# A two-layer transformer trunk: one more pair in block products, weight tiles rounded by DMA, and a new order of the steps

## The chip, the cores and the metric

The kernel runs on one core of one Trainium2 chip. The metric is the device time of one execution in microseconds (us), taken as the median of several executions. The profile is one execution taken by the hardware profiler; its time stands apart, and it lists every instruction of the engines: TensorE (PE, with PEld for its weight loads), VectorE (DVE), ScalarE (ACT), GpSimd (POOL) and SyncE (SP).

## What is computed

Two layers over 256 tokens of 1024 features in float32. Each layer is an attention (the first over 16 heads, causal; the second over 12 heads in three dilated windows), then a squared-ReLU MLP, each followed by a residual and a layer norm:

```python
def sq_relu_mlp(x, w_in, w_out):
    return jnp.square(jax.nn.relu(x @ w_in)) @ w_out      # 1024 -> 4096 -> 1024
...
for i in range(DEPTH):                                     # DEPTH = 2
    mix = moba_attention(...) if i % 2 == 0 else dilated_attention(...)
    h = layer_norm(DEEPNORM_ALPHA * h + mix, ln_mix_g[i], ln_mix_b[i])
    h = layer_norm(DEEPNORM_ALPHA * h + sq_relu_mlp(h, mlp_w_in[i], mlp_w_out[i]), ln_mlp_g[i], ln_mlp_b[i])
```

All weights (about 100 MB) are read from HBM once per execution, and nothing of them is kept between executions.

## The kernel before, in words

**Three products for one.** TensorE multiplies in a rounded form of float32 (fp32r). To keep the accuracy, each operand is split in two: `hi` is the operand rounded to fp32r, `lo` is what is left, `operand - hi`. A product then takes three matmuls: hi·hi, hi·lo and lo·hi. So each 128x1024 weight tile (512 KB) needs work ahead of TensorE: a DMA into a `raw` buffer on SP's queue, a copy that rounds on ACT (`whi<-raw`), and a subtraction on DVE (`wlo<-raw,whi`). There are 7 buffers `raw`, 10 `whi` and 10 `wlo`. Tiles that are named in `FAR` (and in `FAR_W` outside the steps of the MLPs) go without the subtraction: ACT writes `-hi` into `wlo` and a second DMA, on POOL's queue, adds the weights to it from HBM (`far_parts`, L422 to L425).

**The MLP.** The 4096 hidden units are 16 pairs of 128-column tiles. Pairs 0 and 1 are computed at the head (`relu_sq_tok`). For each other pair `p`, two steps `f p 0` and `f p 1` (`do_first`) load a tile of `w_in` each, multiply it, and put the two precision halves together (`half_sum`, L1124); then `square` takes relu and square with two ACT instructions. Then comes the second factor, for which a pair is of one of two kinds:

- A plain pair (`o`, or `O`, which splits its activations early) loads two tiles of `w_out` and takes 2 tiles x 2 token halves x 2 column halves x 3 = 24 matmuls of 128x512 (`do_out`, `mm_rows`).
- A pair in block products (`a`, or `A`, which makes its sums early) takes seven products of blocks in place of eight (Winograd's form of Strassen's scheme), 7 x 3 = 21 matmuls of 128x512 (`do_duo`, `mm_duo`). For this DVE makes four sums of activation blocks (`duo_sums`, L749 on 128x128) and four sums of weight blocks (`load_duo`, L749 on 128x512), and splits the sums like other operands. For a pair in `BY_DMA` two of the four weight sums are one adding DMA of POOL (L698). Its second half runs at the step `b`.

After the last block pair, step `z` (`combine`) adds the partial products to the residual; the pairs behind `z` are the tail, whose products are held back and ordered so that the layer norm of one token half lies beside the products of the other.

**What sets the order.** The program doesn't issue instructions as it is written. Each operation is recorded with a cost, and a list scheduler (`Plan.order`) fixes the order of each engine's queue; the strings `STEPS` give the order in which the MLP's steps are recorded. Buffers that hold finished activations until their step comes are called cells (`CELLS`, `BIG`: parts of attention's tiles that lie idle in the MLP).

On the chip each engine works through its queue in order. POOL's queue holds the adding DMAs and also one small power function per layer norm (`rstd`, L1009), so a DMA that waits there holds up a layer norm behind it.

The pairs in block products are, before: 10 in the first MLP (2, 3, 4, 6, 7, 8, a, c, d, e in hexadecimal) and 11 in the second (2, 3, 4, 5, 6, 7, a, b, c, d, e).

Of the kernel before, what the change touches and what calls it, by code (L numbers as in the profile page):

```python
# [7 lines left out]
F32 = mybir.dt.float32  # L8
# [3 lines left out]
ALU = mybir.AluOpType  # L12
# [29 lines left out]
)  # L42
BY_DMA = ({2, 6, 8, 14}, {2, 5, 6, 10, 14})
FAR = (
    {("f", 7, 0), ("f", 10, 1), ("f", 12, 0), ("f", 12, 1), ("f", 14, 1), ("o", 1, 1), ("s", 6, 0), ("s", 10, 0)},
    {("f", 2, 1), ("f", 7, 0), ("f", 11, 0), ("f", 14, 1), ("s", 10, 0), ("s", 14, 0)},
)
FAR_W = {0, 12, 14, 16, 21, 32, 34, 35, 36, 39, 43, 48, 53, 57}
GB_AT, MASK_AT = "fc1", "f21"
SQUARES = ("AAAAAAAAAAAAAAAA", "AAAAAAAAAAAAAAAA")  # L50


def kinds_of(i):
    at = {int(x[1], 16): x[0] for x in STEPS[i].split() if x[0] in "oOaA"}
    return ["sS"["aA".index(at[p])] if at[p] in "aA" else at[p] for p in range(DFF // 256)]
# [89 lines left out]
class Plan:  # L145
# [52 lines left out]
    def order(self):  # L198
# [40 lines left out]
        def start_of(o):  # L239
# [9 lines left out]
            for tag, bs in need.items():  # L249
# [8 lines left out]
                s = max(s, sorted(slots[tag])[len(bs) - 1])  # L258
# [3 lines left out]
        while len(done) < total:  # L262
# [64 lines left out]
DMA_ISSUE, DMA_FETCH, DMA_LANDS, DMA_RING = 1.0, 2.0, 8.4, 6  # L327
# [20 lines left out]
def tile_trunk(  # L348
# [73 lines left out]
    def far_parts(raw, hi, lo, src, keys):  # L422
        op("ACT", act(1024, sbuf=True), lambda: nc.scalar.activation(hi.t, raw.t, AF.Copy), keys, [(hi, 0)])  # L423
        op("ACT", act(1024, sbuf=True), lambda: nc.scalar.activation(lo.t, f32(hi.t), AF.Copy, scale=-1.0), [(hi, 0)], [(lo, 0)])  # L424
        op("POOL", DMA_ISSUE, lambda: nc.gpsimd.dma_start(lo.t, src, accum_op=ALU.add), (), [(lo, 0)], xfer=P * 1024 * 8)  # L425

    def load_far(src):

        w = W()
        w.raw = mk([P, 1024], F32, "raw", NRAW)  # L430
        w.hi = mk([P, 1024], F32R, "whi", NHI)
        w.lo = mk([P, 1024], F32R, "wlo", NLO)
        dma(lambda: w.raw.t, src, (), [(w.raw, 0)], P * 1024 * 4)
        far_parts(w.raw, w.hi, w.lo, src, [(w.raw, 0)])
        return w
# [3 lines left out]
    def load_w(src):  # L439
        loads[0] += 1  # L440
        return (load_far if loads[0] - 1 in FAR_W else load_near)(src)

    def load_near(src, n=1024):
        w = W()
        w.raw = mk([P, 1024], F32, "raw", NRAW)
        w.hi = mk([P, 1024], F32R, "whi", NHI)
        w.lo = mk([P, 1024], F32R, "wlo", NLO)
        dma(lambda: w.raw.t[:, :n], src[:, :n], (), [(w.raw, 0)], P * n * 4)
        split(
            n, lambda: w.raw.t[:, :n], lambda: w.hi.t[:, :n], lambda: w.lo.t[:, :n],  # L450
            [(w.raw, 0)], [(w.hi, 0)], [(w.lo, 0)], sbuf=True,
        )
        return w

# [205 lines left out]
    def duo_sums(u, cells):  # L660

        t, c0, _ = u
# [14 lines left out]
    def load_duo(pair, single, by_dma, far):  # L677
# [8 lines left out]
        def wide(t, src=None):  # L686
            h, l = [mk([P, 1024], F32R, tag, n) for tag, n in (("whi", NHI), ("wlo", NLO))]
            if src is not None:
                far_parts(t, h, l, src, [(t, 0), (t, 1)])
                return [(h, l, c, 0) for c in (0, 512)]  # L690
            split(1024, lambda: t.t, lambda: h.t, lambda: l.t, [(t, 0), (t, 1)], [(h, 0)], [(l, 0)], sbuf=True)
# [3 lines left out]
        w3, w2 = wide(y, pair[:, 1024:] if far else None)  # L695
# [9 lines left out]
        w5, w7 = wide(x)  # L705
        tt(512, y0, y0, x0, ALU.add, yk[:1] + xk[:1], yk[:1])
        tt(512, y1, y1, y0, ALU.add, yk, yk[1:])
        w6, w4 = wide(y)
# [431 lines left out]
    def relu_sq_tok(ps, m, ahi, alo):  # L1140
# [5 lines left out]
        t = slice(m * P, (m + 1) * P)  # L1146
        keys = [(j, m) for j in range(4)]
        split(
            512, lambda: pt.t.rearrange("p (j s) -> p j s", j=4), lambda: ahi.t[:, :, t], lambda: alo.t[:, :, t],
# [3 lines left out]
    class Mlp:  # L1153
# [17 lines left out]
        def rest(self, between):  # L1171
# [12 lines left out]
            nduo = sum(k in "sS" for k in kinds)  # L1184
# [443 lines left out]
```

## Time and profile before

| | |
|---|---|
| median of 3 executions | 546.9 us (546.07 to 547.66) |
| the profiled execution | 548.12 us, of which the span from the first to the last instruction is 546.3 us |
| granted TensorE clock, mean | 0.996 |
| busy in the span: PE, DVE, ACT, POOL | 537.5, 476.1, 389.8, 41.7 us |
| DMAs moved | 125.03 MB |
| DMAs issued by SP for `w_in` and `w_out` | 64 and 64 |
| DMAs issued by POOL | 37 |

How to read it: the first attention runs to about 105 us of the span, the first MLP to about 290, the second attention to about 360, and the second MLP to 539; the last layer norm and the stores follow. A busy PE is one that has matmuls in flight. The chain of waits follows the end of the program back, at each step to what released the instruction; in a list of groups, a row gives line, engine, operation, tiles (written <- read), shape and count, then busy time in us and the mean of one in ns, then idle time just before them.

### The profile page before, as it was taken

What the parts mean: (1) busy time and instruction counts of PE and PEld (TensorE: products, weight loads), DVE (VectorE), ACT (ScalarE), POOL (GpSimd) and SP (SyncE); (2) the same over time, 40 slices, a digit from 0 to 9 for tenths busy, and PEclk for the clock granted to TensorE, in tenths of its full rate; (3) what the DMA queues carried; (4) which work ended last, traced back from release to release, by engine and by line L of the source; (5) the groups of instructions that cost most, each with busy time, mean ns of one, the idle gap of its engine ahead of it and who ended that gap; (6) DMA issues with size and microseconds to landing.
All of it is one profiled execution on the core that took longest, in us unless ns stands there. A gap on an engine that the chain in (4) does not pass through costs nothing.

```text
span 546.3 us, 8734 instructions
## 1 busy us (share of the span) xinstructions
PE 537.5 (98%) x3172; PEld 458.5 (84%) x3172; DVE 476.1 (87%) x846; ACT 389.8 (71%) x613; POOL 41.7 (8%) x52
## 2 busy tenths in 40 slices
PE   9999999999999999999999999999999999999994
PEld 7989888888888878888888889888888888888884
DVE  6679998897899899899857789879889899899997
ACT  6558999278799768798645558746876997877530
POOL 0000010010001000100011000110010100100001
PEclk9999999999999999999999999999999999999998
DMA  8987787929869879979998756865894989885602
GB/s 331 343 328 242 190 196 197 382 88 308 229 155 237 279 220 288 225 182 324 338 252 224 253 179 173 246 201 138 277 278 118 227 280 268 261 202 178 215 24 78
DMA packets 35611, 125.03 MB, mean 229 GB/s; under 512 B 3952, under 2 KB 4848, under 8 KB 35568
## 3 DMA queue, kind: packets, MB, share of 16 engines
q1 hardware_dynamic: 29664, 104.35, 55.9%
q0 software_dynamic: 5328, 19.40, 19.7%
q10 hardware_dynamic: 576, 0.72, 0.4%
q8 instruction: 25, 0.41, 0.3%
q14 instruction: 18, 0.15, 0.1%
HBM read 123.40 MB, written 1.05 MB: 228 GB/s over the span
## 4 chain that ended last, share of the span: by engine, by line
PE 94%; DVE 2%; DMA 2%; ACT 0%; issue 0%; POOL 0%; DVEq 0%; POOLq 0%; ACTq 0%
PE acc L417 59%; PE tp L417 32%; PE tp L890 3%; DMA raw<-in_win_dram 2%; DVE wlo L413 1%; ACT whi L408 0%; DVE raw L749 0%; POOL rstd L1004 0%; DVE tok L756 0%; DVEq L1622 0%; DVE ta L749 0%; DVE ta L413 0%; DVE pt L413 0%; DVE bst L1035 0%; ACT ta L1127 0%
## 5 line engine op out<-in xcount | busy, mean ns | idle before, releaser
L413 DVE TENSOR_TENSOR wlo<-raw,whi 128x1024 fp32r<-128x1024 f32 (+2 forms) x200 | 222.8, 1137 | 22.1 <-ACT whi L408 20.2
L408 ACT ACTIVATE whi<-raw 128x1024 fp32r<-128x1024 f32 (+2 forms) x198 | 191.0, 995 | 49.8 <-PE acc L417 14.4
L417 PE MATMUL acc<-xs,whi 128*128 128x512 f32 (+1 forms) x496 | 113.4, 374 | 1.1 <-DVE q0lo L749 1.1
L417 PEld LDWEIGHTS acc<-xs,whi 128*128 128x128 f32 x496 | 87.1, 191 | 17.8 <-DVE q0lo L749 1.5
L417 PEld LDWEIGHTS acc<-xs,wlo 128*128 128x128 f32 x448 | 60.0, 191 | 3.5 <-issue 0.2
L417 PE MATMUL acc<-xs,wlo 128*128 128x256 f32 x448 | 62.5, 283 | 0.0
L417 PE MATMUL tp<-xs,whi 128*128 128x512 f32 x224 | 56.3, 392 | 0.0
L417 PE MATMUL acc<-whi,ahi 128*128 128x512 f32 (+1 forms) x130 | 49.7, 392 | 0.0
L417 PEld LDWEIGHTS tp<-xs,whi 128*128 128x128 f32 x224 | 40.4, 189 | 7.3
L417 PE MATMUL acc<-wlo,ahi 128*128 128x512 f32 (+1 forms) x109 | 42.3, 388 | 0.0
L423 ACT ACTIVATE whi<-raw 128x1024 fp32r<-128x1024 f32 x28 | 29.5, 1053 | 16.4 <-PE acc L417 15.3
L417 PE MATMUL acc<-whi,alo 128*128 128x512 f32 (+1 forms) x108 | 39.3, 388 | 0.0
L417 PEld LDWEIGHTS tp<-xs,wlo 128*128 128x128 f32 x224 | 30.5, 190 | 2.1
L417 PE MATMUL tp<-xs,wlo 128*128 128x256 f32 x224 | 31.5, 283 | 0.0
L424 ACT ACTIVATE wlo<-whi 128x1024 fp32r<-128x1024 f32 x28 | 29.6, 1058 | 0.4
L417 PE MATMUL acc<-whi,xs 128*128 128x512 f32 (+1 forms) x112 | 29.0, 364 | 0.0
L417 PEld LDWEIGHTS acc<-whi,ahi 128*128 128x128 f32 x130 | 24.4, 188 | 5.0 <-issue 0.3
L749 DVE TENSOR_TENSOR ta<-acc,ta 128x256 f32<-128x256 f32 x41 | 17.0, 421 | 12.1 <-ACT ta L777 8.7
L417 PE MATMUL tp<-whi,xs 128*128 128x512 f32 x80 | 25.4, 396 | 0.0
L417 PE MATMUL acc<-whi,ta 128*128 128x512 f32 (+1 forms) x72 | 24.5, 384 | 0.0
L417 PEld LDWEIGHTS acc<-whi,alo 128*128 128x128 f32 x108 | 20.3, 188 | 4.2
L417 PEld LDWEIGHTS acc<-wlo,ahi 128*128 128x128 f32 x109 | 20.5, 188 | 3.8
(246 smaller groups left out, 947.8 us busy)
## 6 DMA issues: line engine op xcount, KB each, us to landing
raw<-in_win_dram SPq DMA_DIRECT2D x64, 512.0 KB, 5.7
raw<-in_wout_dram SPq DMA_DIRECT2D x64, 512.0 KB, 6.1
raw<-in_wqk_dram SPq DMA_DIRECT2D x22, 512.0 KB, 8.9
raw<-in_wo_dram SPq DMA_DIRECT2D x14, 512.0 KB, 5.3
wlo<-in_win_dram POOLq DMA_DIRECT2D x10, 512.0 KB, 9.2
raw<-in_wout_dram POOLq DMA_DIRECT2D x9, 512.0 KB, 8.5
raw<-in_wv_dram SPq DMA_DIRECT2D x8, 512.0 KB, 5.4
wlo<-in_wqk_dram POOLq DMA_DIRECT2D x7, 512.0 KB, 9.2
```

Of the source, the lines that this page charges most:

```text
L408: op("ACT", act(n, sbuf=sbuf), lambda: nc.scalar.activation(hi(), src(), AF.Copy), r, whi)
L413: lambda: nc.vector.tensor_tensor(lo(), src(), f32(hi()), op=ALU.subtract), list(r) + list(whi), wlo,
L417: nc.tensor.matmul(out_ap, lhsT, rhs, start=start, stop=stop)
L423: op("ACT", act(1024, sbuf=True), lambda: nc.scalar.activation(hi.t, raw.t, AF.Copy), keys, [(hi, 0)])
L424: op("ACT", act(1024, sbuf=True), lambda: nc.scalar.activation(lo.t, f32(hi.t), AF.Copy, scale=-1.0), [(hi, 0)], [(lo, 0)])
L749: op("DVE", dve(n) + extra, lambda: nc.vector.tensor_tensor(out_ap(), a(), b(), op=alu), r, w)
L890: nc.tensor.transpose(ps.t[:, c : c + P], src(), ident.t)
```

## The change

- The first MLP takes pairs 3, 4, 5, 6, 7, 8, 9, a, b, c, d in block products (11), the second takes 2, 4, 5, 6, 8, 9, a, b, c, d, e (11). Three of them are of a new kind `M`: like `A`, with two of their cells in the buffer `m1` (attention's mask), which is loaded later than before. A kind `G` is added too and is not used.
- A tile in `CAST` or `CAST_W` gets its `hi` from a DMA of POOL that rounds on the way (`cast_in`); ACT's copy goes. There are 42 such tiles. A tile in `FAR` or `FAR_W` gets its `lo` from ACT's `-hi` and an adding DMA as before. A tile in both (15) has no `raw` buffer and no DMA of SP. Three adding DMAs add a sum of weight blocks and read it from SBUF (`wlo<-raw`).
- `BY_DMA` shrinks from 4 and 5 pairs to 2 and 1. `TWICE` would take all four weight sums by DMA; no pair is in both sets, so it doesn't act.
- Seven pairs (`D` in `SQUARES`) take relu and square in one DVE instruction in place of two of ACT.
- `STEPS` has a new order in both MLPs; the planner hands out buffers first in, first out, and has two other constants for DMAs of POOL.

```diff
-    "f20 fd0 f21 f30 fc0 f40 f31 f41 fa0 fd1 f80 fa1 f90 A4 f50 f81 f51 Aa Ad fc1 ba f70 bd b4 A2 fb0 f91 "
+    "f40 f80 f30 f31 f41 fa0 fa1 f81 A3 fd0 fc0 f90 b3 fd1 A4 fc1 M8 f20 fb0 b4 f91 ff0 f70 f71 b8 Aa ff1 "
...
-BY_DMA = ({2, 6, 8, 14}, {2, 5, 6, 10, 14})
+BY_DMA = ({9, 10}, {5})
...
-FAR_W = {0, 12, 14, 16, 21, 32, 34, 35, 36, 39, 43, 48, 53, 57}
-GB_AT, MASK_AT = "fc1", "f21"
-SQUARES = ("AAAAAAAAAAAAAAAA", "AAAAAAAAAAAAAAAA")
+FAR_W = {13, 17, 28, 30, 38, 55, 57}
+GB_AT, MASK_AT = "f91", "bb"
+CAST = (
+    {("f", 2, 1), ("f", 4, 1), ("f", 5, 1), ("f", 12, 0), ("f", 13, 0), ("o", 14, 1)},
...
+CAST_W = {12, 13, 15, 17, 18, 24, 27, 28, 30, 33, 34, 36, 37, 40, 42, 43, 45, 47, 53, 54, 55, 56}
+TWICE = ({5, 12, 13}, {4, 6, 7, 9, 11, 12, 13, 14})
+SQUARES = ("AAAADAAAADDAAAAD", "AAAADAAAAAAAADAD")
...
-                s = max(s, sorted(slots[tag])[len(bs) - 1])
+                s = max([s] + slots[tag][: len(bs)])
...
-    def far_parts(raw, hi, lo, src, keys):
-        op("ACT", act(1024, sbuf=True), lambda: nc.scalar.activation(hi.t, raw.t, AF.Copy), keys, [(hi, 0)])
+    def cast_in(hi, src):
+        op("POOL", DMA_ISSUE, lambda: nc.gpsimd.dma_start(hi.t, src), (), [(hi, 0)], xfer=P * 1024 * 4 - 1)
+
+    def add_in(lo, hi, src, keys=()):
         op("ACT", act(1024, sbuf=True), lambda: nc.scalar.activation(lo.t, f32(hi.t), AF.Copy, scale=-1.0), [(hi, 0)], [(lo, 0)])
-        op("POOL", DMA_ISSUE, lambda: nc.gpsimd.dma_start(lo.t, src, accum_op=ALU.add), (), [(lo, 0)], xfer=P * 1024 * 8)
+        op("POOL", DMA_ISSUE, lambda: nc.gpsimd.dma_start(lo.t, src(), accum_op=ALU.add), keys, [(lo, 0)], xfer=P * 1024 * 8)
...
+    def load_as(src, far, cast):
 
         w = W()
-        w.raw = mk([P, 1024], F32, "raw", NRAW)
+        if not (far and cast):
+            w.raw = mk([P, 1024], F32, "raw", NRAW)
         w.hi = mk([P, 1024], F32R, "whi", NHI)
         w.lo = mk([P, 1024], F32R, "wlo", NLO)
-        dma(lambda: w.raw.t, src, (), [(w.raw, 0)], P * 1024 * 4)
-        far_parts(w.raw, w.hi, w.lo, src, [(w.raw, 0)])
+        if not (far and cast):
+            dma(lambda: w.raw.t, src, (), [(w.raw, 0)], P * 1024 * 4)
+        if cast:
+            cast_in(w.hi, src)
+        else:
+            op("ACT", act(1024, sbuf=True), lambda: nc.scalar.activation(w.hi.t, w.raw.t, AF.Copy), [(w.raw, 0)], [(w.hi, 0)])
+        if far:
+            add_in(w.lo, w.hi, lambda: src)
+        else:
+            low_part(w.raw, w.hi, w.lo, [(w.raw, 0)])
         return w
...
+    def low_part(raw, hi, lo, keys):
+        tt(1024, lambda: lo.t, lambda: raw.t, lambda: f32(hi.t), ALU.subtract, [*keys, (hi, 0)], [(lo, 0)])
...
-                    n = {"O": 2, "S": 4}.get(kinds[p], 0)
-                    u = cells.take(F32) if not n else (mk([P, 512], F32, "ta", NTA), 0, 0)
-                    homes = [cells.take(F32R, True) for _ in range(n)]
+                    n = {"O": 2, "S": 4, "M": 2}.get(kinds[p], 0)
+                    u = cells.take(F32) if kinds[p] in "os" else (mk([P, 512], F32, "ta", NTA), 0, 0)
+                    homes = [h for tag in {"G": ("g", "b"), "M": ("m1",)}.get(kinds[p], ()) for h in cells.spot(tag)]
+                    homes += [cells.take(F32R, True) for _ in range(n)]
```

Two places show what this does to the queues. The first is POOL's queue where the second MLP begins, around the two `rstd` of the layer norm ahead of it. `whi<-in_win` is a rounding DMA of a tile of `w_in`, `wlo<-in_win` an adding one, `in_wout` is `w_out`. Before:

```order
L425 DMA wlo_793_4102<-in_win_dram 128x1024
L1009 TENSOR_TENSOR rstd_779_4182<-rstd_779_4182,expo_3_100 128x1
L425 DMA wlo_817_4196<-in_win_dram 128x1024
L1009 TENSOR_TENSOR rstd_801_4245<-rstd_801_4245,expo_3_100 128x1
L698 DMA raw_919_4482<-in_wout_dram 128x1024
L425 DMA wlo_922_4628<-in_wout_dram 128x1024
```

And now:

```order
L429 DMA whi_785_4003<-in_win_dram 128x1024
L433 DMA wlo_783_4083<-in_win_dram 128x1024
L433 DMA wlo_789_4103<-in_win_dram 128x1024
L429 DMA whi_805_4132<-in_win_dram 128x1024
L1039 TENSOR_TENSOR rstd_776_4168<-rstd_776_4168,expo_3_100 128x1
L429 DMA whi_812_4176<-in_win_dram 128x1024
L429 DMA whi_824_4188<-in_win_dram 128x1024
L1039 TENSOR_TENSOR rstd_797_4228<-rstd_797_4228,expo_3_100 128x1
L429 DMA whi_871_4348<-in_win_dram 128x1024
L429 DMA whi_896_4464<-in_win_dram 128x1024
L433 DMA wlo_872_4514<-in_win_dram 128x1024
```

One adding DMA stood between the two `rstd`; now two rounding DMAs stand there, and a further one right ahead of the first.

The second place is DVE's queue near the end of the first MLP. Rows `wlo<-raw,whi` take the low part of a weight tile, rows `raw<-raw` sum weight blocks, `tok` is the residual. Before, plain pairs come last here:

```order
L413 TENSOR_TENSOR wlo_569_2964<-raw_567_2855,whi_568_2944 128x1024
L413 TENSOR_TENSOR wlo_572_2974<-raw_570_2872,whi_571_2952 128x1024
L413 TENSOR_TENSOR wlo_575_2984<-raw_573_2903,whi_574_2966 128x1024
L413 TENSOR_TENSOR wlo_580_2993<-raw_578_2915,whi_579_2986 128x1024
L413 TENSOR_TENSOR ta_577_3005<-pt1_368_2100,ta_576_2959 128x512
L413 TENSOR_TENSOR wlo_583_3017<-raw_581_2929,whi_582_3000 128x1024
L749 TENSOR_TENSOR ta_584_3015<-tp_371_2255,ta_584_3015 128x512
```

And now, from the last but one block pair on:

```order
L779 TENSOR_TENSOR raw_552_2745<-raw_552_2745,raw_551_2718 128x512
L419 TENSOR_TENSOR wlo_556_2928<-raw_562_2797,whi_555_2884 128x512
L779 TENSOR_TENSOR wlo_565_2938<-raw_563_2815,whi_564_2895 128x1024
L419 TENSOR_TENSOR q0hi_497_2950<-ta_495_2782,v_496_2930 128x512
L419 TENSOR_TENSOR ta_561_2952<-ta_557_2888,ta_560_2940 128x384
L779 TENSOR_TENSOR raw_552_2745<-raw_552_2745 128x512
L779 TENSOR_TENSOR wlo_567_2961<-raw_551_2718,whi_566_2942 128x1024
L779 TENSOR_TENSOR raw_562_2797<-raw_562_2797 128x512
L779 TENSOR_TENSOR raw_562_2797<-raw_562_2797,raw_563_2815 128x512
L779 TENSOR_TENSOR wlo_569_2980<-raw_552_2745,whi_568_2963 128x1024
L779 TENSOR_TENSOR raw_563_2815<-raw_563_2815,raw_562_2797 128x512
L779 TENSOR_TENSOR raw_563_2815<-raw_563_2815 128x512
```

The sums of weight blocks, four to a pair, stand close to the end of the MLP now, between the low parts. Over the whole program, by the queues: DVE goes from 810 rows to 840, ACT from 563 to 504, POOL's DMAs from 37 to 72, SP's from 203 to 188. TensorE's matmuls of 128x512 go from 1725 to 1722, the others stay.

More of the change, by code (lines that the diff above doesn't have):

```diff
@@ L623, in __init__ @@
             self.half = []
+            self.gone = set()
         def take(self, dtype, wide=False):
@@ L684, in load_duo, with wide @@
         dma(lambda: y.t, pair[:, 1024:], (), yk, P * 1024 * 4)
-        def wide(t, src=None):
+        def wide(t, part, src, again):
             h, l = [mk([P, 1024], F32R, tag, n) for tag, n in (("whi", NHI), ("wlo", NLO))]
[L688 to L691, printed above, removed]
+            keys = [(t, 0), (t, 1)]
+            if part in cast:
+                cast_in(h, src)
+            else:
+                op("ACT", act(1024, sbuf=True), lambda: nc.scalar.activation(h.t, t.t, AF.Copy), keys, [(h, 0)])
+            if part in far:
+                add_in(l, h, again, [] if src is not None else keys)
+            else:
+                low_part(t, h, l, keys)
             return [(h, l, c, 0) for c in (0, 512)]
         split(512, x0, part(hi, q * 512, 512), part(lo, q * 512, 512), xk[:1], [(hi, q)], [(lo, q)], sbuf=True)
-        w3, w2 = wide(y, pair[:, 1024:] if far else None)
+        w3, w2 = wide(y, 0, pair[:, 1024:], lambda: pair[:, 1024:])
         if by_dma:
@@ L704, in load_duo @@
         yield w2, w3, (hi, lo, q * 512, q)
[L705 to L708, printed above, removed]
+        w5, w7 = wide(x, 1, None, lambda: x.t)
+        if by_dma > 1:
+            op(
+                "POOL", DMA_ISSUE, lambda: nc.gpsimd.dma_start(y1(), pair[:, :512], accum_op=ALU.add), yk[1:], yk[1:],
+                xfer=P * 512 * 8,
+            )
+            op("POOL", DMA_ISSUE, lambda: nc.gpsimd.dma_start(y.t, x.t, accum_op=ALU.add), xk + yk, yk, xfer=P * 1024 * 8)
+        else:
+            tt(512, y0, y0, x0, ALU.add, yk[:1] + xk[:1], yk[:1])
+            tt(512, y1, y1, y0, ALU.add, yk, yk[1:])
+        w6, w4 = wide(y, 2, None, lambda: y.t)
         yield w5, w7, w6, w4
@@ L1146, in relu_sq_tok @@
         t = slice(m * P, (m + 1) * P)
+        quads = lambda tile: tile.rearrange("p (j s) -> p j s", j=4)
+        if alo is None:
+            op(
+                "ACT", act(512), lambda: nc.scalar.activation(quads(ahi.t)[:, :, t], quads(pt.t), AF.Copy), [pt],
+                [(ahi, j) for j in range(4)],
+            )
+            return
         keys = [(j, m) for j in range(4)]
         split(
-            512, lambda: pt.t.rearrange("p (j s) -> p j s", j=4), lambda: ahi.t[:, :, t], lambda: alo.t[:, :, t],
+            512, lambda: quads(pt.t), lambda: ahi.t[:, :, t], lambda: alo.t[:, :, t],
             [pt], [(ahi, k) for k in keys], [(alo, k) for k in keys],
@@ L1160, in head @@
             self.ws = [[load_w(win[i][c * 4 + j]) for j in range(4)] for c in range(nx)]
-            self.chunks = {c: act_tiles() for c in range(nx)}
+            whole = kinds_of(i)[0] in "sS"
+            self.chunks = {c: (mk([P, 1024], F32, "ahi", 3), None) if whole else act_tiles() for c in range(nx)}
             self.half(0)
@@ L1183, in rest @@
             prods = []
-            nduo = sum(k in "sS" for k in kinds)
+            nduo = sum(k in "sSGM" for k in kinds)
             single = [None]
@@ L1219, in do_first @@
                     square(held[p][0], SQUARES[i][p])
-                    if kinds[p] in "OS":
+                    if kinds[p] in "OSGM":
                         ready(p)
@@ L1226, in do_pair @@
             def do_pair(p):
-                if p < 2 * nx:
+                if kinds[p] in "os" and p in held:
+                    ready(p)
+                if p < 2 * nx and kinds[p] == "o":
                     gets = [rows_of(*chunks[p // 2], p % 2 * 2 + k) for k in range(2)]
                 else:
-                    if kinds[p] in "os":
-                        ready(p)
                     gets = held[p]
@@ L1257, in do_duo @@
                 a11, a12, a22, s1, s2, s3, s4 = do_pair(p)
-                weights = load_duo(wout[i][p], (*single[0], q), p in BY_DMA[i], ("s", p, 0) in FAR[i])
+                weights = load_duo(wout[i][p], (*single[0], q), (p in BY_DMA[i]) * (1 + (p in TWICE[i])), *[
+                    {n for n in range(3) if ("s", p, n) in parts[i]} for parts in (FAR, CAST)
+                ])
                 if q:
@@ L1295, in combine @@
                 tt(512, lambda: z1.t[:, hi], w(p5), lambda: z1.t[:, hi], ALU.add, [(z1, 1), p5], [(z1, 1)])
+            if chunks[0][1] is None:
+                for p in range(2 * nx):
+                    homes = [cells.take(F32R, True) for _ in range(4)] if kinds[p] == "S" else []
+                    held[p] = (chunks[0][0], p * 512, 2 * p), homes
+                    taken[p] = homes
+                    if homes:
+                        ready(p)
             late_ = False
@@ L1570, in _layout @@
         for p, kind in enumerate(kinds_of(i)):
-            if kind in "sS":
+            if kind in "sSGM":
                 t = wo[i, p // 2, p % 2, 1]
```

58 lines of the change are left out of this document (29 added, 29 removed), and 6 rows, old and new, of the table STEPS.

## The prediction

> **What bounds the kernel now.** I read the page's totals first, then what TensorE waits for, then the chain of waits, then busy time by stage. On the page:
>
> ```profile
> span 546.3 us, 8734 instructions
> PE 537.5 (98%) x3172; PEld 458.5 (84%) x3172; DVE 476.1 (87%) x846; ACT 389.8 (71%) x613; POOL 41.7 (8%) x52
> ```
>
> TensorE is busy for all but 8.8 us of the span. The list of TensorE's own waits has two rows:
>
> ```profile
> PE acc L417 <- DVE q0lo L749: 1.1, 1, 1.1
> PE tp L417 <- PEq L1613: 0.8, 1, 0.8
> ```
>
> One of them is the start. The other, 1.1 us, is the only time in the program's middle at which TensorE had nothing to do, for a result of DVE. The chain of waits (start, length, what) shows where it lies and where the end lies:
>
> ```profile
> 172.44 10.45 DMA raw<-in_win_dram
> ...
> 194.51 0.35 DVE q0lo L749
> ...
> 194.90 3.06 PE acc L417 x16
> ...
> 217.40 0.68 PE tp L417 x3
> 218.08 2.77 PE acc L417 x16
> ...
> 539.34 0.44 DVE bst L1035
> ```
>
> So up to 539.3 us TensorE sets the end, but for one detour: a load of a `w_in` tile that took 10.45 us, then ACT and DVE work until 194.9, in the first MLP. The 7 us behind 539.3 are the last layer norm and the stores, whose code doesn't change. This fixes the best that can come: less TensorE work, and the one wait.
>
> The stages (busy us of each engine and instruction count in each stretch, then granted clock, DMA share and GB/s), first the two MLPs whole, then parts of them:
>
> ```profile
> 122.00:287.00 165.00, 163.94 (x832) 139.27 (x832) 144.97 (x220) 128.76 (x180) 14.03 (x16) 1.00 0.86 252
> 378.00:539.00 161.00, 161.00 (x833) 137.96 (x833) 149.22 (x231) 115.39 (x166) 9.61 (x11) 1.00 0.71 208
> ```
> ```profile
> 160.00:200.00 40.00, 38.94 (x198) 32.86 (x197) 36.89 (x60) 33.47 (x48) 3.47 (x4) 1.00 0.78 228
> ...
> 378.00:420.00 42.00, 42.00 (x240) 36.85 (x240) 37.82 (x62) 31.37 (x48) 1.75 (x2) 1.00 0.80 230
> 420.00:460.00 40.00, 40.00 (x204) 34.15 (x204) 37.01 (x59) 37.71 (x56) 3.48 (x4) 1.00 0.88 248
> 460.00:500.00 40.00, 40.00 (x204) 34.12 (x203) 36.73 (x61) 31.32 (x47) 3.45 (x4) 1.00 0.81 227
> 500.00:539.00 39.00, 39.00 (x190) 32.83 (x189) 37.66 (x52) 15.00 (x17) 0.93 (x1) 1.00 0.36 122
> ```
>
> DVE (third busy figure) is the next engine behind TensorE: 88% in the first MLP, 93% in the second, 97% in its last 39 us, there without a wait of TensorE. ACT has room, DMA some.
>
> **The change part by part.**
>
> *Products.* A plain pair takes 24 matmuls of 128x512 and a block pair 21. Block pairs go from 10 to 11 in the first MLP and stay 11 in the second, so three matmuls go. The chain has three of them in 0.68 us at 217.40. They lie on TensorE, which sets the end: -0.7 us, certain if TensorE still sets it.
>
> *The wait at 194 us.* The new order of steps may take it away (-1.1) or leave one of its kind.
>
> *DVE and ACT.* The groups by shape give busy us and mean ns of one:
>
> ```profile
> L413 DVE TENSOR_TENSOR wlo<-raw,whi 128x1024 fp32r<-128x1024 f32 x171 | 205.0, 1220 | 19.9 <-ACT whi L408 18.5 <-PE acc L417 0.5
> L749 DVE TENSOR_TENSOR raw<-raw,raw 128x512 f32<-128x512 f32 x33 | 22.6, 686 | 0.3
> L749 DVE TENSOR_TENSOR ta<-ta,ta 128x128 f32<-128x128 f32 x34 | 9.8, 287 | 0.4
> L756 DVE SCALAR_TENSOR_TENSOR tok<-tok,ta 128x512 f32<-128x512 f32 x6 | 4.1, 686 | 0.1
> L413 DVE TENSOR_TENSOR alo<-ta,alo 128x384 fp32r<-128x384 f32 x6 | 3.3, 553 | 0.3 <-ACT alo L408 0.3
> ```
> ```profile
> L408 ACT ACTIVATE whi<-raw 128x1024 fp32r<-128x1024 f32 x171 | 175.9, 1056 | 47.4 <-PE acc L417 14.4 <-PE tp L417 11.1 <-DVE raw L749 11.1
> L1136 ACT ACTIVATE ta<-ta 128x512 f32<-128x512 f32 x21 | 13.3, 631 | 0.6
> ```
>
> By the queues, between the layer norms around the first MLP, DVE gets 9 more operations of 128x512 (weight sums that POOL no longer takes, and splits), 4 of 128x128, one of 128x384 and 4 squares, and loses one low part: 9 x 0.69 + 4 x 0.29 + 0.55 + 4 x 0.69 - 1.2 = +9.4 us. In the second MLP it gets 8 of 128x512 and 3 squares and loses 3 low parts: 5.5 + 2.1 - 3.6 = +4.0. ACT loses 12 copies of 1.06 and 7 of 0.63 in the first (-17 us) and 6 and 6 in the second (-10). The two attentions give DVE six low parts more (+7) and take 24 copies from ACT (-25). DVE's work lies beside TensorE's, and costs nothing while DVE keeps ahead. Cover in the first MLP: 165.0 - 145.0 = 20 us of idle DVE, of which 9.4 go; in the second 11.8, of which 4.0 go. Part of that idle was a wait for ACT's copies (18.5 us over the program, in the first row above), and ACT is earlier now. So I cost it at nothing, with 0 to 2.5 us as its range (below).
>
> *DMA.* Queue and kind with packets, MB and share of the 16 DMA engines' time; then issues by kind with median us to landing, and POOL's time to issue one (idle ahead of it behind the bar):
>
> ```profile
> q1 hardware_dynamic: 29664, 104.35, 55.9%
> q0 software_dynamic: 5328, 19.40, 19.7%
> ```
> ```profile
> raw<-in_win_dram SPq DMA_DIRECT2D x64, 512.0 KB, 5.7
> ...
> wlo<-in_win_dram POOLq DMA_DIRECT2D x10, 512.0 KB, 9.2
> ```
> ```profile
> L425 POOL DMA_DIRECT2D wlo<-in_win_dram x10 | 8.7, 870 | 96.5 <-ACT wlo L424 62.5 <-ACT sc L1127 17.0 <-DVE wlo L413 17.0
> ```
>
> A plain 512 KB load takes 0.559 x 546.3 / 104.35 x 0.524 = 1.53 us of all 16 DMA engines, an adding one 0.197 x 546.3 / 37 = 2.91. No rounding DMA is in the trace; I bound it by these two, 1.53 to 2.91 of the engines and 5.7 to 9.2 us to landing, and take the lower: it reads one source and writes once like the plain load, whereas the adding one also reads its destination. A tile that is rounded and added to is ready 5.7 to 9.2, then 1.06 on ACT (a pass over a tile, as in the copies above), then 9.2: 16 to 19.5 us after its issue. What hides that is the store of ten `whi` tiles: one `w_in` tile feeds 2.77 us of TensorE (218.08), ten of them 28 us. At 5.7 or at 9.2 it fits, so nothing is added to the sum.
>
> *POOL's queue at a layer norm.* Ahead of the second MLP, two rounding DMAs stand between the two `rstd`:
>
> ```profile
> 364.11 0.93 POOL L1009 TENSOR_TENSOR rstd<-rstd,expo 128x1 f32<-128x1 f32 x1 [8.68 <-PE acc L417]
> 367.34 0.89 POOL L425 DMA_DIRECT2D wlo<-in_win_dram  x1 [2.31 <-ACT wlo L424]
> 370.54 0.93 POOL L1009 TENSOR_TENSOR rstd<-rstd,expo 128x1 f32<-128x1 f32 x1 [2.31 <-DVE rstd L1007]
> ```
>
> Two issues need 1.8 of the 5.5 us from 365.04 to 370.54. Costed at nothing; if a `whi` buffer comes free only then, `rstd` is late by 0.9 per issue, and with it the transposes that TensorE takes next.
>
> *Sum.* Against the profiled execution: 548.12 (span 546.3 and 1.8 outside) - 0.7 = 547.4 with a wait of the old one's size left somewhere, 546.3 without any. The median of the runs is 1.2 below the profiled time: **546.2** and 545.1. I take 546.2, because DVE gets denser just where it was late.
>
> **The rivals.** A difference of 0.3%, 1.6 us here, is about what a measurement of this kernel can tell from no change.
>
> *All of the gain.* Both terms hold, and the relief of ACT keeps DVE ahead: 546.9 - 0.7 - 1.1 = 545.1, just beyond 0.3%. For it: the second MLP before ran at 93% DVE without a wait. Against: no slack is left for a late load. Two terms of 0.7 and 1.1 are all that this trace has to give.
>
> *DVE paces the first MLP.* DVE needs 145.0 + 9.4 = 154.4 us there, and TensorE's work is 163.94 - 0.7 = 163.3; DVE would have to run at 95% throughout. In the stretch of the wait, 160 to 200, it got to 36.89 / 40 = 92.2%. At that pace 154.4 us take 167.5, against 165.0 before: +2.5 us, 549.4. It decides once DVE can't get above 94.5%. Against it: ACT's relief, and 97% at 500 to 539.
>
> *DMA runs full in the second MLP.* There 17 rounding DMAs come in, one adding DMA more, and 8 plain loads less: 17c + 2.9 - 12.2. At c = 1.53 that is 17 us, at 2.91 it is 40. From 378 to 500 the DMA engines idle for 0.20 x 42 + 0.12 x 40 + 0.19 x 40 = 20.8 us. At 40 some 19 us are left over, and of the 25 idle us behind 500 about half can still serve tiles in time: 7 us late, 546.2 + 7 = 553. It decides from c = (20.8 + 9.3) / 17 = 1.8 on without that half, 2.5 with it. Loads that come late like the one of 10.45 us would show it.
>
> The Trainium skill bears on this rival from two sides. "DMA: Bandwidth & Descriptors", section "Anatomy of one DMA — SWDGE (gpsimd) path", gives a DMA of POOL 2.0 us plus its bytes over 436 GB/s, by which 512 KB would land in 3.2 us and take 1.2 of the engines; with that the rival has no case (11 us more into 20.8 idle), and the sum stays. The adding DMAs of this trace, at 9.2 us to landing, don't agree, so I keep the bounds from the rows. The same page, section "SWDGE vs HWDGE vs iDMA", says that each DMA engine takes turns between the queues of the two kinds. That speaks against the change: each further DMA of POOL stretches SP's loads. The load of 10.45 us against a median of 5.7 is of that form, though the trace doesn't show that an adding DMA caused it.
>
> *That it doesn't do what it says.* `TWICE` meets no pair of `BY_DMA`, so that part is empty; the rest is in the queues.
>
> **How the numbers follow.** My forecast (546.2; its own range 545.3 to 548.5 from no wait up to a few short ones) gets 0.49, all of the gain 0.23, DVE as pace 0.18, DMA full 0.10. Faster by over 0.3% is the second: 0.23; within 0.3% the first: 0.49; slower the other two: 0.28. The range reaches down to 544.9, below which little of the second case lies, and up to 550.5: it takes in DVE's case with a microsecond more, and leaves out DMA's and the edges, some 2 in 10.
>
> **What would show it.** Right: TensorE's busy time falls by about 0.7 to 537, its waits stay at a microsecond or two, the chain stays on TensorE, DVE's busy time rises by about 20 to some 497 (9.4 + 4.0 + 7), ACT's falls by some 50. Rounding DMAs land nearer to 5.7 than to 9.2. The forecast is wrong if TensorE waits for DVE or for a `raw` or `whi` load for more than 3 us in an MLP, if DMA share goes over 0.95 in 378 to 500, or if TensorE waits behind `rstd`. All of the gain shows as no wait at all but the start's.

## The result and the profile after

The changed kernel takes 552.7 us (median of 5, 551.58 to 554.16) beside 546.6 of the kernel before in the same rounds (546.07 to 547.66): 1.0116 times as long, with a 95% interval of 1.0105 to 1.0127. That is slower by 6.1 us. The forecast was 546.2 with a range of 544.9 to 550.5, so the time lies above the range.

The profiled execution after took 551.58 us, of which the span is 549.5. The page's totals:

```profile
span 549.5 us, 8749 instructions
PE 537.4 (98%) x3169; PEld 456.8 (83%) x3169; DVE 493.0 (90%) x877; ACT 342.8 (62%) x559; POOL 58.4 (11%) x87
```

TensorE is as busy as before, with three matmuls fewer; DVE has 17 us more, ACT 47 us less, POOL 17 us more. What is new are TensorE's waits (us in total, times, longest; the second row is the program's start):

```profile
PE acc L423 <- DVE ta L779: 4.1, 3, 2.2
PE tp L423 <- PEq L1664: 0.8, 1, 0.8
```

By the starts of its matmuls the three of the first row lie at 192 us (0.6), 224 (2.3) and 463 (1.8), 4.6 us together. All are for DVE. The chain of waits shows what DVE was late for; its rows around the three waits (start, length, what):

```profile
181.23 9.95 DMA whi<-in_win_dram
...
209.38 0.96 ACT wlo L432
210.34 0.35 issue
210.69 0.37 POOL wlo L433
...
211.78 13.37 DMA raw<-in_wout_dram
...
225.17 0.69 DVE raw L779
225.86 0.35 DVE ta L779
...
226.25 1.88 PE acc L423 x7
...
451.36 2.37 DVE wlo L779 x2
...
453.74 9.58 DMA raw<-in_wout_dram
...
463.41 0.21 DVE raw L779
...
465.09 3.07 PE acc L423 x16
```

The reader is to see two different things, beside the short wait at 192, whose chain goes back to a rounding DMA of 9.95 us. At 224, in the first MLP, the chain goes from DVE back through a transfer of 13.37 us to POOL's queue. In the second MLP it goes back through a load of 9.58 us to DVE itself, which freed the `raw` buffer only at 453.7. DVE's own queue at the first place (start, length, operation, idle just before it):

```profile
221.76 0.69 DVE L779 TENSOR_TENSOR raw<-raw 128x512 f32<-128x512 f32 x1
225.17 0.69 DVE L779 TENSOR_TENSOR raw<-raw,raw 128x512 f32<-128x512 f32 x1 [2.72 <-DMA raw<-in_wout_dram]
```

DVE works through its queue in order, so all that stands behind this weight sum is 2.72 us late, the `ta` that TensorE waits for among it. The transfer of 13.37 us is one of the adding DMAs that sum weight blocks for a pair in `BY_DMA` (L721). On POOL's queue after:

```profile
200.53 0.55 POOL L429 DMA_DIRECT2D whi<-in_win_dram  x1 [6.92 <-PE acc L423]
209.48 0.85 POOL L433 DMA_DIRECT2D wlo<-in_win_dram  x1 [8.39 <-ACT ta L1157]
210.69 0.85 POOL L433 DMA_DIRECT2D wlo<-in_win_dram  x1 [0.36 <-ACT wlo L432]
211.78 0.85 POOL L721 DMA_DIRECT2D raw<-in_wout_dram  x1 [0.25 <-issue]
```
```profile
DMA to landing us min/median/max: 7.5/7.7/13.4
```

The last row is for the three DMAs of L721. Two other adding DMAs were issued 2.3 and 1.1 us ahead of the one at 211.78; they landed after 8.0 and 10.7 us:

```profile
DMA to landing us min/median/max: 8.0/9.4/10.7
```

So the three landed one behind the other, at 217.5, 221.4 and 225.2 us. In the kernel before, no such sum had another DMA close ahead of it in the queue; L698 is its line there:

```profile
169.81 0.86 POOL L425 DMA_DIRECT2D wlo<-in_win_dram  x1 [4.48 <-ACT wlo L424]
174.93 0.86 POOL L698 DMA_DIRECT2D raw<-in_wout_dram  x1 [4.26 <-DVE ta L749]
195.60 0.87 POOL L425 DMA_DIRECT2D wlo<-in_win_dram  x1 [19.81 <-ACT wlo L424]
214.69 0.86 POOL L698 DMA_DIRECT2D raw<-in_wout_dram  x1 [18.22 <-DMA raw<-in_wout_dram]
```
```profile
DMA to landing us min/median/max: 5.4/8.5/9.0
```

Nothing had been issued for 5 us ahead of the first of them, for 19 us ahead of the second, and for at least 4 us ahead of any of the nine, and none of the nine took over 9.0 us. The stages of the changed kernel (busy us of PE, PEld, DVE, ACT, POOL, then clock, DMA share, GB/s), and the DMAs of POOL (its queue with packets, MB and share; then two kinds with median us to landing):

```profile
122.00:287.00 165.00, 162.45 (x821) 137.25 (x820) 151.18 (x234) 115.76 (x163) 16.46 (x23) 1.00 0.84 253
378.00:539.00 161.00, 159.41 (x819) 135.97 (x817) 149.86 (x233) 106.34 (x155) 16.48 (x23) 1.00 0.76 227
```
```profile
q0 software_dynamic: 10368, 37.75, 27.6%
...
whi<-in_win_dram POOLq DMA_DIRECT2D x20, 512.0 KB, 6.8
wlo<-in_win_dram POOLq DMA_DIRECT2D x17, 512.0 KB, 8.0
```

DVE is busy for 92% and 93% of the two MLPs, and the DMA engines for 84% and 76%: over a whole MLP neither is full. Where the weight sum came late, the DMA engines were (a share can pass 1, since a transfer counts where it starts):

```profile
215.00:220.00 5.00, 5.00 (x28) 4.12 (x27) 4.92 (x11) 4.13 (x8) 0.00 (x0) 1.00 1.06 245
220.00:225.00 5.00, 4.10 (x22) 3.20 (x20) 2.28 (x4) 1.53 (x3) 0.85 (x1) 1.00 1.03 314
```

### The profile page after: what moved, and what is told of

It reads as the page before. It is cut to its first block, busy times and chain, and to the rows that moved or that the text cites. A ratio compares the mean times of both kernels' runs of the same rounds, so it can differ in the third digit from the quotient of the medians.

```text
span 549.5 us, 8749 instructions
## 1 busy us (share of the span) xinstructions
PE 537.4 (98%) x3169; PEld 456.8 (83%) x3169; DVE 493.0 (90%) x877; ACT 342.8 (62%) x559; POOL 58.4 (11%) x87
## 4 chain that ended last, share of the span: by engine, by line
PE 76%; DVE 10%; DMA 9%; issue 2%; ACT 1%; POOL 0%; DVEq 0%; POOLq 0%; ACTq 0%
PE acc L423 49%; PE tp L423 24%; DMA raw<-in_wout_dram 7%; DVE wlo L779 5%; PE tp L920 3%; DMA whi<-in_win_dram 2%; DVE raw L779 2%; DVE tok L786 1%; DVE ta L779 1%; ACT whi L710 1%; DMA raw<-in_xw_dram 0%; ACT whi L453 0%; DVE wlo L419 0%; DVE bst L1092 0%; POOL rstd L1034 0%
## 5 line engine op out<-in xcount | busy, mean ns | idle before, releaser
L779 DVE TENSOR_TENSOR wlo<-raw,whi 128x1024 fp32r<-128x1024 f32 x173 | 206.3, 1219 | 8.4 <-ACT whi L453 7.8
L423 PE MATMUL acc<-xs,whi 128*128 128x512 f32 (+1 forms) x560 | 129.1, 375 | 4.3 <-DVE ta L779 4.1
L453 ACT ACTIVATE whi<-raw 128x1024 fp32r<-128x1024 f32 x93 | 96.1, 1053 | 43.6 <-PE acc L423 20.3
L710 ACT ACTIVATE whi<-raw 128x1024 fp32r<-128x1024 f32 x65 | 67.7, 1054 | 22.8 <-DVE raw L779 15.9
L423 PE MATMUL acc<-whi,ahi 128*128 128x512 f32 x128 | 49.3, 394 | 0.0
L423 PE MATMUL tp<-xs,whi 128*128 128x512 f32 x160 | 40.2, 392 | 0.0
L423 PEld LDWEIGHTS tp<-xs,whi 128*128 128x128 f32 x160 | 28.9, 189 | 5.2
L779 DVE TENSOR_TENSOR raw<-raw,raw 128x512 f32<-128x512 f32 x41 | 28.2, 688 | 5.2 <-DMA raw<-in_wout_dram 4.6
L779 DVE TENSOR_TENSOR raw<-raw 128x512 f32<-128x512 f32 x41 | 28.2, 688 | 0.7
L433 POOL DMA_DIRECT2D wlo<-in_win_dram x17 | 14.7, 863 | 125.8 <-ACT wlo L432 61.9
L906 ACT ACTIVATE sc<-sc,mx 128x256 f32<-128x256 f32 (+2 forms) x40 | 19.8, 502 | 8.0 <-DVE mx L896 8.0
```

The source lines that it names most:

```text
L423: nc.tensor.matmul(out_ap, lhsT, rhs, start=start, stop=stop)
L433: op("POOL", DMA_ISSUE, lambda: nc.gpsimd.dma_start(lo.t, src(), accum_op=ALU.add), keys, [(lo, 0)], xfer=P * 1024 * 8)
L779: op("DVE", dve(n) + extra, lambda: nc.vector.tensor_tensor(out_ap(), a(), b(), op=alu), r, w)
L906: lambda: nc.scalar.activation(e(), e(), AF.Exp, bias=bias(), scale=-1.0, accum_out=total()), r, w,
```

## The experiments

In the expectations, before and changed stand for the two kernels of this study. Two theories stood at the start. L: transfers land late, because the rounding DMAs fill POOL's queue and the DMA engines. D: the new steps leave DVE too dense to keep a lead over TensorE, whatever the transfers do.

**Which part of the change: four kernels.** The first takes the changed code with all tables of before, which leaves only the planner's own changes. The second takes the MLPs' tables of before and the attentions' tiles as changed, the third the opposite, the fourth has no rounding DMA.

```diff
 e1:  STEPS, BY_DMA, FAR, FAR_W, GB_AT, MASK_AT, SQUARES of before
      CAST, TWICE = (set(), set()), (set(), set());  CAST_W = set()
 e2:  as e1, with CAST_W and FAR_W as changed
 e3:  as changed, with FAR_W of before and CAST_W = set()
 e4:  as changed, with CAST = (set(), set()) and CAST_W = set()
```

> The changed code with all the tables of before (steps, kinds, FAR, BY_DMA, squares; no rounding DMA): what is left of the change is the planner's first-in-first-out buffers and its constant for an adding DMA (8.8 in place of 8.4). Theory L (late transfers: the rounding DMAs make POOL's queue slow, adding DMAs and loads land late, and DVE, in order, waits for them): 546 to 547.5. Theory D (dense DVE work: the new steps with more weight sums on DVE leave it no lead over TensorE, whatever the transfers): 546 to 547.5. A third reading, that the planner's new rules make the order worse, would give 550 or more.

> The tables of before in both MLPs, but the rounding and adding DMAs of the change everywhere else (CAST_W and FAR_W: 22 rounding DMAs). The changed kernel's trace has no wait of TensorE outside the MLPs. Theory L: up to 2 us lost, 546.5 to 549, as POOL's queue carries casts into the MLPs' heads alone. Theory D: nothing, 546 to 547.5.

> The change in both MLPs, with the adding DMAs of before elsewhere and no rounding DMA there. Theory L: 20 rounding DMAs are left in the MLPs, where the waits are: 550 to 553. Theory D: 551 to 553. Both say that nearly all of the loss stays; if it goes (under 548.5), it came from the attention stages and both are wrong.

> The changed kernel without any rounding DMA: all 42 tiles are loaded by SP and rounded by ACT as before; steps, kinds, adding DMAs and squares as changed. Theory L: POOL's queue is free again, the waits for late transfers go: 545.5 to 548. Theory D: the waits stay: 551 to 554, and more if ACT's 44 us of copies come in addition.

Measured, beside 546.4 for before: e1 546.5 (ratio 0.999 to 1.0009), e2 549.0 (1.0029 to 1.0059), e3 558.9 (1.0201 to 1.0269), e4 552.3 (1.0092 to 1.0122). The planner's changes cost nothing. In e1's profile TensorE waits for nothing but the start:

```profile
span 544.6 us, 8736 instructions
```
```profile
PE tp L420 <- PEq L1661: 0.8, 1, 0.8
```

e1 came as both theories had it, e2 at the top of L's range, e4 within D's, and e3 beyond both. Without any rounding DMA the time is what it is with 42 of them, which speaks against L as it was put. But the parts don't add up: e2 and e3 lose 2.6 and 12.6 us, the whole change 6.1. Each of these kernels is planned anew, so each has its own order and its own waits; e4 has seven of 0.4 to 0.8 us where the changed kernel has three. They say that the planner's changes are harmless, and nothing safe on the rest. So the next kernels keep the changed kernel's order on every engine, which a planner that is told nothing of the cut allows, and do less on the chip.

**The same order, less work: five kernels.** e5 and e6 shorten the 82 weight sums of DVE from 512 columns to 64 and 256; e7 shortens POOL's 30 adding DMAs from 1024 to 128; e9 shortens only the three of these that sum weight blocks; e10 is e5 and e7 at once. So each leaves out part of the sums that the reference needs.

```diff
 e5 (and with 256, e6), one of the four sums:
-            tt(512, x0, x0, x1, ALU.add, xk, xk[:1])
+            tt(512, part(x, 0, 64), part(x, 0, 64), part(x, 512, 64), ALU.add, xk, xk[:1])
 e7:
-        ... nc.gpsimd.dma_start(lo.t, src(), accum_op=ALU.add)
+        ... nc.gpsimd.dma_start(lo.t[:, :128], src()[:, :128], accum_op=ALU.add)
 e7 and e9:
-        ... nc.gpsimd.dma_start(x.t, pair[:, 512:1536], accum_op=ALU.add)
+        ... nc.gpsimd.dma_start(x.t[:, :128], pair[:, 512:640], accum_op=ALU.add)
```

> The queues of every engine keep the rows and the order of the changed kernel; the 82 weight sums of block pairs on VectorE go over 64 columns in place of 512, so most of each weight sum is left out. That takes about 82 x 0.55 = 45 us of work off VectorE, and nothing off the DMAs. D (VectorE is too dense to have a lead): TensorE's waits for VectorE in the MLPs go, the chain is TensorE's again, and the time is 545 to 546.5. L (transfers land late because of POOL's queue): VectorE still stands in order behind the same late loads; the waits stay at some 2 us each and the time stays above 550.

> Same queues again; the 82 weight sums go over 256 columns in place of 512, so half of each weight sum is left out: about 82 x 0.3 = 25 us off VectorE. D: VectorE's need in an MLP falls below TensorE's by more than the loads are late, and most of the loss goes: 546 to 549. L: 550 to 552.5, as changed.

> Same queues; each adding DMA of POOL (27 for low parts and 3 for weight sums) adds 128 of its 1024 columns, so 7/8 of these sums are left out. That takes about 30 x 2.5 us of all 16 DMA engines away and makes these transfers land sooner, with VectorE's work unchanged. L: the late transfers of the chain (13.37 us for an adding DMA in the first MLP) get short and the time falls to 546 to 548. D: VectorE is as dense as before and the time stays within 1 us of 552; at most the first MLP's wait of 2.3 us, whose chain runs through an adding DMA, goes, which would make it 550.

Measured: e5 549.6 (1.0037 to 1.0084), e6 548.9 (1.0031 to 1.0064), e7 548.2 (1.0023 to 1.0054), beside 546.6. Neither theory holds alone: only e6's time is in a range, D's 546 to 549, and its wait is still there, 1.6 us at 223 behind a transfer of 13.05 us. In e5 DVE is busy for 456.5 us, 36.5 less, and yet the wait at 224 us stands at 2.2 us (totals, TensorE's wait, chain; the profiled execution took 551.7 us, the longest of e5's four):

```profile
PE 538.7 (98%) x3169; PEld 459.0 (84%) x3169; DVE 456.5 (83%) x877; ACT 342.7 (62%) x559; POOL 58.4 (11%) x87
```
```profile
PE acc L423 <- DVE ta L779: 3.1, 3, 2.0
```
```profile
211.97 13.77 DMA raw<-in_wout_dram
```

The transfer of the weight sum takes 13.77 us here, so D falls for the first MLP. In the second MLP the wait of 1.8 us shrinks to 0.5 in e5 and goes in e6: DVE's work has a part there, through the `raw` buffers that it frees late. In e7, with short adding DMAs, both long waits go (0.6 and 0.9 are left, at 209 and 470), with DVE's work as in the changed kernel. So DVE isn't the whole cause in the second MLP either. The load that took 9.58 us there was issued right behind an adding DMA (at 453.74 and 453.69); in e7, where that DMA is short, it lands after

```profile
DMA to landing us min/median/max: 6.9/6.9/6.9
```

So the late start of the load, which hangs on DVE, and its long transfer both have a part in this wait.

> The queues keep the changed kernel's order; only the three adding DMAs of POOL that sum weight blocks for a block pair (two in the first MLP, one in the second) add 128 of their 1024 columns, so 7/8 of these three sums are left out. A (each MLP has its own late thing: in the first the adding DMA of a weight sum, in the second a load of a raw buffer that VectorE freed too late): the wait of 2.3 us at 224 us goes and the wait of 1.8 us at 463 stays, 549 to 550.5. B (POOL's transfers as a whole load the DMA engines, and no single one matters): no change, 551.5 to 553.

> Both cuts at once on the changed kernel's order: the 82 weight sums of VectorE over 64 of 512 columns, and all 30 adding DMAs of POOL over 128 of 1024 columns. A: the two causes make up the whole loss, no wait over 0.6 us is left in an MLP, and the time is that of the forecast or below: 545 to 546.5. If something else has a part (the rounding DMAs that land after 10 us, the order of TensorE's own work): 547 or more, with a wait at 192 us or in an attention.

Measured: e9 548.3 (1.0016 to 1.0042), e10 547.9 (1.0016 to 1.0037). Three shorter DMAs out of 72 take 4.4 of the 6.1 us away, so theory A is right on the first MLP, though the time is a little below its range: of the wait at 224 us 0.4 is left. The wait at 460 us stays in e9 (1.6 us), as A had it, and is down to 0.4 in e10. With both cut, 1.3 us and a wait of 0.7 at 209 remain: A's forecast of 545 to 546.5 was too low, and something else has a part. Rows of e9: the landing of the three DMAs of L721, now with an eighth of the bytes, and one of them in the chain of waits:

```profile
DMA to landing us min/median/max: 2.9/3.6/11.6
```
```profile
210.50 11.56 DMA raw<-in_wout_dram
```

The other two land in 2.9 and 3.6 us. This one still takes 11.6, with 64 KB. So it isn't its bytes that take the time, but what stands ahead of it. In e7, where the two adding DMAs ahead of it are as short, it lands after 2.6 us:

```profile
DMA to landing us min/median/max: 2.6/2.7/4.8
```

**Planned anew: two kernels.** e8 tells the planner longer landing times for POOL's DMAs; e11 takes all weight sums to DVE. Both do the whole computation.

```diff
 e8:
-DMA_ISSUE, DMA_FETCH, DMA_LANDS, DMA_CASTS, DMA_RING = 1.0, 2.0, 8.8, 7.0, 6
+DMA_ISSUE, DMA_FETCH, DMA_LANDS, DMA_CASTS, DMA_RING = 1.0, 2.0, 12.0, 10.0, 6
 e11:
-BY_DMA = ({9, 10}, {5})
+BY_DMA = (set(), set())
```

> All work as in the changed kernel, but the planner reckons 12 and 10 us for an adding and a rounding DMA of POOL to land, in place of 8.8 and 7.0, and orders the queues anew. L: with transfers counted at what they take under load, fewer results come late: 548 to 550. D: the work of VectorE is the same, and another order moves its waits without taking them away: 550 to 554.

> BY_DMA is empty: all weight sums go to VectorE, six more of 128x512 (4.1 us), the three adding DMAs of weight sums go, and the planner orders anew. The whole computation is done. A: the late adding DMA is gone, and with it the wait at 224 us, but VectorE is denser: 549 to 552. B: 551.5 to 554.

Measured: e8 568.3 (1.0373 to 1.0421), e11 557.1 (1.0153 to 1.0203): beyond what either theory gave them. The late adding DMA is gone in e11, and the longest wait is 3.8 us, at another place. Five plans of the new steps (changed, e3, e4, e8, e11) lie between 552 and 568 us; such runs can't tell a cause.

**One DMA moved: two kernels.** Q says that the weight sum lands late because it queues behind the two adding DMAs issued ahead of it; T says that the bytes in flight share the DMA engines in whatever order. Both kernels compute everything, and differ from the changed one in POOL's queue alone, at this one place.

```diff
         ops = self.order()
 e12: ahead of the two POOL DMAs that stood before it
+        o = self.hurry[1]      # the second adding DMA of L721
+        for q in [q for q in ops[: ops.index(o)] if q.eng == "POOL" and q.xfer][:-3:-1]:
+            ops.remove(q)
+            ops.insert(ops.index(o) + 1, q)
 e13: as early as what it needs allows, which is ahead of one of the two
+        for o in self.hurry:
+            ops.remove(o)
+            ops.insert(1 + max(ops.index(p) for p in o.preds), o)
```

The loop of e13 runs over all three adding DMAs of L721; by the traces only the second of them changes its place.

> The whole computation; every queue keeps the changed kernel's order but for one place in POOL's: the adding DMA that sums weight blocks of the second BY_DMA pair of the first MLP (issued at 211.8 us in the changed kernel, landing 13.4 us later) goes ahead of the two adding DMAs of low parts that stood before it. Q (it lands late because it queues behind those two; with 1/8 of its size it still took 11.6 us): it lands about 9 us after an issue at 210.5, ahead of VectorE's need at 222.4; the wait of 2.3 us at 224 us goes, that at 463 stays, 548 to 550. T (the transfers themselves share the DMA engines, whatever their order): the wait stays or moves to the two low parts, 551 to 553.

> The same, but the adding DMA goes ahead of only one of the two. Q: about half of the queueing goes, landing some 11 us after an issue at 210.7, just ahead of VectorE's need at 222.4: wait at 224 us under 1 us, 548.5 to 551. T: 551 to 553.

Measured: e12 549.0 (1.0032 to 1.0057), e13 547.5 (1.0012 to 1.0031, 11 executions), beside 546.6. One swap of two neighbours in POOL's queue takes 5.2 of the 6.1 us away, more than either Q or T gave it. Of this the wait at 224 us is 2.3. The other two waits are smaller as well in e13's profile (none at 192, 0.9 at 460), although nothing in the queues was changed there; how much of that the swap did isn't shown. POOL's queue, the landing of the three weight sums (L724 there) and TensorE's wait for DVE in e13:

```profile
208.55 0.85 POOL L436 DMA_DIRECT2D wlo<-in_win_dram  x1 [7.79 <-ACT ta L1161]
209.86 0.85 POOL L724 DMA_DIRECT2D raw<-in_wout_dram  x1 [0.46 <-PE acc L426]
210.45 1.14 POOL L436 DMA_DIRECT2D wlo<-in_win_dram  x1
```
```profile
DMA to landing us min/median/max: 5.9/7.4/11.5
```
```profile
PE acc L426 <- DVE ta L783: 0.7, 1, 0.7
```

It is issued 1.9 us earlier and lands 11.5 us later, at 221.4, just ahead of the 222.4 at which DVE had come to it in the changed kernel. No wait is left in the first MLP. The adding DMA that now stands behind it lands after 14.8 us instead, and TensorE doesn't wait for it. In e12, ahead of both, all three weight sums land fast, and by the chain another transfer is late instead, a load that SP issued at 216.4:

```profile
DMA to landing us min/median/max: 6.2/7.2/7.9
```
```profile
216.38 14.60 DMA raw<-in_wout_dram
```

It makes TensorE wait for 1.2 us at 233, and 1.4 at 462 stays. So Q is right on the weight sum: with two, one and no adding DMA close ahead it took 13.4, 11.5 and at most 7.9 us. T is right in so far as the delay didn't vanish: it went to an adding DMA in e13, and partly to a load of the other queue in e12. No kernel here beats the one before; e1 is level with it.

## Why the prediction was wrong, point by point

**The step that failed** is the one on DVE: "I cost it at nothing, with 0 to 2.5 us as its range". Measured were 4.6 us of waits of TensorE for DVE. The reason given for nothing was that DVE's work has cover, 20 us of idle in the first MLP. That cover is real, and the amounts were about right: DVE's busy time rose by 16.9 us (about 20 in the working), ACT's fell by 47.0 (some 50). In the first MLP it wasn't DVE's work that cost: e5 takes 36.5 us of it away, and the long wait stays. What cost there was a weight sum that landed 13.37 us after its issue, behind two other adding DMAs. In the second MLP it was a load that started only when DVE had freed its buffer and then took 9.58 us. A sum over an MLP can't see one transfer on which an in-order queue stands still for 2.72 us.

**POOL's queue** was looked at in one place, at the layer norm, and costed at nothing there; that was right, as TensorE never waits behind `rstd` in the changed kernel. It wasn't looked at inside the first MLP. The order of the queues had it: where each weight sum of L698 had no other DMA within 4 us ahead of it in POOL's queue, the one at 211.8 stands right behind two adding DMAs of `wlo`, which were held for ACT for 8.4 us and then came together. The row on which the cost rested was the median landing of an adding DMA, 9.2 us, and the one that counts took 13.4.

**Rounding DMAs** were bounded by 1.53 and 2.91 us of the DMA engines. After: (0.276 x 549.5 - 30 x 2.91) / 42 = 1.53, the lower end, if an adding one still costs 2.91. The 20 of `w_in` land after 6.8 us by the median, nearer to 5.7 than to 9.2; the medians of the other groups go from 7.0 to 9.8. That nothing was added for their own transfers isn't shown to be right: the wait of 0.6 us at 192 goes back to one of them that took 9.95 us, issued 0.6 us behind a weight sum. It isn't in every execution, as e12 and e13, whose queues are the same up to there, have no wait at 192. e4 can't settle it, because it is planned anew.

**DMA full in the second MLP** had 553, and 552.7 came out. Only the price was near, and that by luck. Its sign was to be a DMA share over 0.95 in 378 to 500. The share there is 0.84, against 0.83 before, and the larger part of the loss is in the first MLP:

```profile
378.00:500.00 122.00, 120.41 (x638) 103.50 (x637) 111.49 (x181) 88.18 (x134) 13.57 (x19) 1.00 0.84 248
```

What it had right is that a load which comes late would show: the one of 9.58 us did, though the DMA engines were full only around it (1.06 from 460 to 465).

**DVE as the pace of the first MLP** had 549.4 by a stage in which DVE can't get above 94.5%. DVE did get less there, 151.2 / 165 = 92%, but because it stood waiting; in e13, with the same queue, it has 93% at 154.25 busy us in this stretch, and TensorE has no wait there:

```profile
122.00:287.00 165.00, 164.92 (x836) 140.24 (x835) 154.25 (x240) 116.73 (x164) 17.27 (x24) 1.00 0.83 259
```

That is close to the 154.4 us which the prediction worked out for DVE's need. The rival fails, and by the reason given against it.

**The products** are three matmuls fewer, 1722 against 1725, worth 0.7 us by the chain. TensorE's busy time doesn't show it: 537.4 after against 537.5, but 536.7 in e1 and 536.6 in e13. Of e13's 0.9 us over before, the remaining wait explains 0.9 (by the starts of matmuls, at 460), and 0.2 lie outside the span (2.0 us against 1.8); against them stands the 0.7. Some 0.5 us is in gaps too small to name.

**The wait at 194 us** was taken off twice. The prediction took 1.2 us off the profiled time for the median, and then, in the case with all of the gain, 1.1 for the wait. But the wait most likely was that difference: 51 other executions of before, from the rounds of the experiments, have spans of 544.2 to 545.9 us where the profiled one has 546.3, and e1, whose queues of DVE and POOL are before's up to there, shows no wait at 544.6. So the most that the change could give was 0.7 us, within what can be told from none, and the chance of 0.23 for faster had no case under it.

**The load on SP's queue.** The 1.8 us at 463 come from two things together: DVE frees the `raw` buffer only at 453.7, and the load then takes 9.58 us beside an adding DMA. With less work on DVE (e6) and with short adding DMAs (e7) the wait at 463 is gone. What SP waits for over the whole program (total, times, longest), after and before:

```profile
SPq L410 <- DVE wlo L779: 304.6, 115, 15.8
```
```profile
SPq L404 <- DVE wlo L413: 246.4, 119, 9.7
```

SP stands 58 us longer for DVE to free `raw` buffers, and 40 us less for ACT (22.4 in place of 62.6). The prediction asked what hides a late tile behind the store of `whi` tiles, and not what starts its load.

What stays open: 1.3 us are left in e10 with both causes cut. Its waits (0.7 at 209 and 0.4 at 470) hang on rounding DMAs by the chain, of 8.0 us each; a kernel with the changed order and short rounding DMAs wasn't tried, since the rest of the tile would be read unwritten. And the profiled execution is the shortest of the five: the others are up to 2.6 us longer at granted clocks of 0.989 to 0.995 against 0.998, which fits a stretch at half clock as in the last section, but they left no trace.

## What to carry to other kernels

A median landing time doesn't price a DMA that stands close behind others. Where one engine waits in order for a certain DMA, read the rows ahead of it on the queue that issues it: two large DMAs issued within 2.3 us made this one some 5 us late, and in the kernel in which it changed places with one of them, 5.2 of the 6.1 us were gone. Read the DMA share of that stretch too, not only that of the stage: here 1.06 against 0.84. To find such a cause in a program that a planner orders, keep the order and shrink or move one thing, since each new plan brings its own waits.

## What the runs showed of the hardware

**POOL's DMAs land in the order of issue.** In each of the 15 traces every DMA of POOL lands later than the one issued ahead of it (72 of them in the changed kernel), so a small one can't pass a large one. A weight sum of 64 KB took 11.6 us behind two adding DMAs of 512 KB (e9), where its like took 2.9 and 3.6, and 2.6 behind two of 64 KB (e7). The Trainium skill, "DMA: Bandwidth & Descriptors", section "Two DMAs through the same engine are not ordered", says that within one queue of a DMA engine descriptors start in order. The order of landing in these traces agrees with it; when a descriptor starts, they don't show.

**A wait of 2 us can cost more than itself.** In e5's profile the clock that TensorE was granted fell to half for 3.4 us, 1.0 us after the wait of 2.2 us at 224 (columns as in the stages above):

```profile
220.00:226.00 6.00, 4.37 (x23) 3.42 (x22) 0.85 (x5) 1.95 (x4) 0.85 (x1) 1.00 1.06 312
226.00:231.00 5.00, 4.62 (x17) 4.06 (x18) 4.60 (x6) 4.19 (x5) 0.00 (x0) 0.66 0.67 165
231.00:236.00 5.00, 5.00 (x23) 4.12 (x23) 3.83 (x5) 3.55 (x5) 0.00 (x0) 1.00 0.90 314
```

Matmuls of 128x512 start 427 ns apart there against 227, so about half of the 3.4 us is lost in addition. In e3 half clock set in 1.5 us after a wait of 2.3 us and lasted for 6.8; in e8 a wait of 2.5 us was followed by 6.8 us of it and one of 2.8 by 3.4; in e11 it set in during the wait of 3.8 us and lasted for 6.8. In the changed kernel's profile the wait of 2.3 us had no such sequel, and no wait under 2 us in a trace had one. The Trainium skill, "TensorE: Matmul & The Clock Gate", section "Why this matters for your kernels", sets the bound at gaps of some 3 us; the trace of e5 shows half clock after a wait of 2.2.
